# A two-layer hybrid decoder on one core: dropping the meta tokens behind attention and cutting the remaining 1024 into tiles of 256

## The chip, the cores and the metric

The kernel runs on one core of a Trainium2 chip. TensorE (PE in the profile) multiplies 128 x 128 weights, which it loads first (PEld), with a moving operand of up to 512 columns and writes to PSUM, which has eight banks of 512 fp32 columns. VectorE (DVE), ScalarE (ACT) and GpSimd (POOL) do the rest of the arithmetic; SyncE (SP) only issues transfers here. The metric is the device time of one execution in microseconds (us), as the median of several runs.

## The reference, cut to what matters

The input has 1024 tokens of width 1024; 16 learned meta tokens are put in front, which makes 1040. Layer 0 is a state-space mixer and a convolutional gated network (FFN); layer 1 is a stick-breaking attention and an FFN. The meta tokens are dropped at the very end.

```python
h = jnp.concatenate([jnp.broadcast_to(meta_tokens[None], ...), x], axis=1)      # 1040 tokens
h = h + _ssd_mixer(_rmsnorm(h, ssd_norm[0]), ...)
h = h + _conv_ffn(_rmsnorm(h, ffn_norm[0]), ...)
...
o = _stick_breaking_attention(q, k_shared, v_shared).reshape(b, L, SB_WIDTH)
h = h + o @ sb_w_o[j]
h = h + _conv_ffn(_rmsnorm(h, ffn_norm[layer]), ...)
return _rmsnorm(h, final_norm)[:, N_META:]

def _conv_ffn(u, w_up, conv_w, conv_b, w_down):
    h = _causal_dwconv(u @ w_up, conv_w, conv_b)      # three taps: this token and the two in front
    g, val = jnp.split(h, 2, axis=-1)
    return (jax.nn.silu(g) * val) @ w_down
```

Attention reads keys and values of all 1040 tokens. Behind it only the FFN's convolution looks at other tokens: the two in front. So of the meta tokens only the last two have any effect on the output of layer 1's last steps.

## The kernel before

**Numbers and layout.** The stream is held as eight tiles of 128 features x tokens. Each fp32 product is made of three matmuls on split operands (`mm3`, L148): high x high, high x low, low x high, at lines 151 to 153. A matmul line in the profile is therefore mostly one of these three, and the names of its operands tell the stage.

**Tiles of tokens.** The FFN of both layers works on L = 1040 tokens, in four tiles of `FN` = 260 and in halves of 520. The up projection has a halo of `HB` = 2 tokens, so its matmuls have 262 columns.

**Output projection** (`o_proj`, L1405). The attention output of 8 head pairs is read from DRAM and split (`split` in thirds, `split_half` in halves). For each of eight feature blocks, four tiles of 260 are accumulated over 4 or 6 pairs (`accumulate`, L376), whose end is the DVE add at L383.

**Step into the FFN** (`enter_ffn`, L729). The last pairs are added tile by tile; squares are summed by a matmul with ones (`square_row`, L804) to the norm's factors; the stream goes to DRAM (`hm`); `forms` (L814) makes the seven operand sums that the up projection's fast 2 x 2 matrix scheme needs (seven products instead of eight).

**Up projection** (`up`, L896). 22 blocks; each has two halves of tokens with seven products of 4 x 3 matmuls, a three-tap convolution (`conv`, L269), SiLU, a product and a store of 260 tokens to DRAM (`g`).

**Down projection** (`down`, L969). Sixteen of 22 blocks of hidden rows go through the same seven-product scheme, in two rounds of two sets. For each product, `operands` (L1008) of a set are made on DVE, ACT and POOL one set ahead: sums, then splits (`gl` at L1032, `wl` at L1030). A product has eight PSUM tiles (two tiles of 260 tokens x four feature blocks), which take all eight banks by the list `kinds`; a first pass over all eight with set 0, a second with set 1, and behind each tile of the second pass an add to its accumulator (`add`, L1072: DVE at L1077, ACT at L1075 in round 0 for four of the products). The six rows left over are plain products, tile by tile (L1144 on), and meanwhile DVE runs `sums` (L1043), which puts the seven products together.

**The end** (`finish`, L1428; `finish_tokens`, L1441; `finish_last`, L1467). The final norm and the transpose to token rows run per chunk of up to 116 tokens: `down` calls `after(h, j - 1)` behind tile j, so that tokens 0 to 347 leave behind tile 1, tokens 348 to 779 behind tile 2. The last tile's 260 tokens go in chunks of 96, 96 and 68 through `finish_last`, whose `each` runs behind each feature block of tile 3. Transposes go to banks of the tag `sm`, of which there are three.

**Order.** Behind attention no order is written by hand. A scheduler puts each engine's instructions in order by a simulated timeline; where several are ready, the one that the program traced first goes first. PSUM and SBUF tiles of one tag rotate through its buffers. `keep_in_program_order` (L175) puts an activation-table load behind the instruction that ScalarE was given last.

Of the kernel before, what the change touches and what calls it, by code (L numbers as in the profile page):

```python
# [29 lines left out]
FN = 260  # L30
HB = 2
FW = 264

# [33 lines left out]
class Trunk:  # L67
# [87 lines left out]
    def split(self, t, s, eng=None):  # L155

        nc = self.nc
        hi, lo = self.Q(s + "h", F32R), self.Q(s + "l", F32R)
        for s0, n in TT:
            c = slice(s0, s0 + n)  # L160
            nc.scalar.activation(hi[:, c], t[:, c], AF.Copy)
            (eng or nc.vector).tensor_tensor(lo[:, c], t[:, c], hi[:, c].bitcast(F32), op=ALU.subtract)
        return hi, lo

    def split_half(self, t, s):

        x = self.Q(s, F32R)
        hi, lo = x[:, : L // 2], x[:, QW // 2 : QW // 2 + L // 2]
# [560 lines left out]
    def enter_ffn(self, layer, h, last, pool):  # L729


        nc = self.nc
# [6 lines left out]
        def tile(j, work):  # L739
            ws, ops = last[j // 2]  # L740
            ms[j] = self.sm("ms")
            for f in range(KD):
                self.accumulate(h, f, FN * j, FN, lambda i, f: (ws[i][0][:, f * P : f * P + P], ws[i][1][:, f * P : f * P + P]), ops, HB, next(banks), L // 2 * (j // 2))
                self.square_row(ms[j], h, j, f)
                next(work, None)

        def factors(j):

            c = r[:, HB + FN * j : HB + FN * j + FN]
            b, ps = self.tmp("y")[:, :FN], ms.pop(j)[:, :FN]  # L750
# [9 lines left out]
        def rest():  # L760
            forms.append(form_tiles())
            yield from self.forms(h, r, 1, f"ffn_norm{layer}", forms[1], pool)
# [21 lines left out]
        def store(x):  # L784
            for k in range(KD):
                nc.sync.dma_start(d[k, :, L // 2 * x : L // 2 * (x + 1)], h[k][:, HB + L // 2 * x : HB + L // 2 * (x + 1)])
# [8 lines left out]
        work = self.forms(h, r, 0, f"ffn_norm{layer}", forms[0], pool)  # L795
# [8 lines left out]
    def square_row(self, ms, h, j, f):  # L804

        q = self.tmp("sq")[:, :FN]
        self.nc.scalar.activation(q, h[f][:, HB + FN * j : HB + FN * j + FN], AF.Square)
        self.nc.tensor.matmul(ms[:, :FN], self.ones, q, start=f == 0, stop=f == KD - 1, skip_group_check=True)
# [5 lines left out]
    def forms(self, h, r, t, gain, tiles, pool):  # L814


        nc = self.nc
# [78 lines left out]
    def up(self, layer, w0, forms, rest, pool):  # L896

        nc = self.nc
        tt = nc.vector.tensor_tensor
        N = HB + FN  # L900
        cw, cb = f"ffn_conv_w{layer}", f"ffn_conv_b{layer}"
        d = self.dp.tile([KF, P, L], F32, tag=f"g{layer}", name=f"g{layer}")
# [66 lines left out]
    def down(self, layer, gd, hd, pool, after, each=None):  # L969
# [4 lines left out]
        H, S = D // 2, L // 2  # L974
# [97 lines left out]
        def add(i, f, t, ps, first):  # L1072
            x = acc[i, f][:, FN * t : FN * t + FN]
            if first and i in (1, 5, 6, 7):
                nc.scalar.activation(x, ps[:, :FN], AF.Copy)  # L1075
            else:
                self.last_add = tt(x, x, ps[:, :FN], op=ADD)  # L1077
# [35 lines left out]
        for m in range(0, len(plan), 2):  # L1113
# [3 lines left out]
            if r == 0 and i == 7:  # L1117
                for f in range(KD):
                    nc.sync.dma_start(h[f][:, :L] if f < 4 else h[f][:, half(0)], hd[f] if f < 4 else hd[f, :, half(0)])
# [5 lines left out]
            for x in range(2):  # L1125
# [279 lines left out]
    def o_proj(self, hd, od, pool):  # L1405

        a = self.a
        h = [None] * KD
        first = PAIRS - 2

        def part(p, x):
            t = self.Q("o")[:, : L // 2]
            self.nc.sync.dma_start(t, od[p, :, L // 2 * x : L // 2 * (x + 1)])
            return self.split_half(t, "o")

        ops = [self.split(self.fetch(od[p], "o"), "o") for p in range(first - 2)]
        ops = [ops + [part(p, 0) for p in (first - 2, first - 1)], ops]
        for f in range(KD):
            w = self.load_w(a["w_o_f"][f], first * P)
            h[f] = self.fetch(hd[f], "h", front=HB)  # L1420
# [185 lines left out]
```

## Time and profile before

| what | value |
|---|---|
| median of 3 runs (lowest, highest) | 3010.03 us (3007.62, 3012.0) |
| span of the profiled execution | 3005.5 us |
| median of the runs less that span | 4.5 us |
| TensorE busy, mean granted clock | 2887.2 us (96%), 0.986 |
| VectorE, ScalarE, GpSimd busy | 77%, 55%, 44% |

The profile covers one execution, from its first to its last instruction. The 4.5 us between the span and the median of the runs are taken as what lies around the span; the profiled execution's own time is known only through its span. "Idle before" in a row is the time in which the engine stood still just before these instructions, with the instruction that released it. A row that begins with two times is a start and a duration; a row that begins with a window has for each engine the busy time and in brackets the number of instructions.

### The profile page before, as it was taken

To read this page: it belongs to the slowest core of one execution; us is meant where nothing else is said; L and a number is where in the kernel's file an instruction comes from. 1 tells how busy PE (TensorE), PEld (TensorE's weight loads), DVE (VectorE), ACT (ScalarE), POOL (GpSimd) and SP (SyncE) were. 2 spreads that over 40 slices of the span, in tenths; PEclk is the share of its full clock that TensorE was granted. 3 is DMA by queue.
4 is the path that set the end of the run, shared out by engine and by line. 5 is a ranking of instruction groups with operands and counts; after the bars stand their busy time and mean duration, and the time that the engine had idled before them with its cause. 6 is when DMAs were issued, how large, how long until landed. Compare 5 with 4: busy or idle time off the path is not lost. (4 is left out here: it accounts for less than half of the span.)

```text
span 3005.5 us, 58807 instructions
## 1 busy us (share of the span) xinstructions
PE 2887.2 (96%) x22559; PEld 2776.5 (92%) x22559; DVE 2311.1 (77%) x4073; ACT 1657.7 (55%) x3419; POOL 1308.8 (44%) x1260
## 2 busy tenths in 40 slices
PE   7999999989998999999999999999899999999998
PEld 4999898979998999999999999999798999999998
DVE  5587868886369788778966888888749887888875
ACT  4554545553145556555324888887736556555433
POOL 1254444542335666654343222222343666663441
PEclk9999999999999999999999999999999999999999
DMA  5233333323221222235132222222332222225332
GB/s 162 71 106 90 105 97 103 108 63 138 74 82 56 83 73 79 84 107 178 50 128 81 59 67 57 71 61 56 131 114 71 79 75 82 79 75 181 100 100 64
DMA packets 123482, 273.43 MB, mean 91 GB/s; under 512 B 13728, under 2 KB 53280, under 8 KB 123200
## 3 DMA queue, kind: packets, MB, share of 16 engines
q1 hardware_dynamic: 117824, 258.54, 27.7%
q10 hardware_dynamic: 4112, 6.56, 0.7%
q8 instruction: 178, 2.92, 0.4%
q0 software_dynamic: 1264, 4.57, 0.4%
q14 instruction: 104, 0.85, 0.1%
HBM read 201.25 MB, written 53.45 MB: 85 GB/s over the span
## 5 line engine op out<-in xcount | busy, mean ns | idle before, releaser
L151 PE MATMUL pj<-uh,wh 128*128 128x348 f32 (+2 forms) x1536 | 504.7, 329 | 12.2 <-ACT bk L609 6.2
L152 PE MATMUL pj<-ul,wh 128*128 128x348 f32 (+2 forms) x1536 | 497.9, 324 | 0.0
L153 PE MATMUL pj<-uh,wl 128*128 128x348 f32 (+2 forms) x1536 | 495.2, 323 | 0.0
L151 PE MATMUL p<-bh,fh 128*128 128x262 f32 x1408 | 403.5, 287 | 6.6 <-DVE c L276 4.6
L153 PE MATMUL p<-bh,fl 128*128 128x262 f32 x1408 | 403.1, 287 | 3.6 <-POOL fl L882 3.6
L152 PE MATMUL p<-bl,fh 128*128 128x262 f32 x1408 | 402.6, 286 | 0.1
L882 POOL TENSOR_TENSOR fl<-x,fh 128x1024 fp32r<-128x1024 f32 x88 | 212.6, 2417 | 269.4 <-ACT fh L881 176.6
L152 PE MATMUL p<-bl,wh 128*128 128x262 f32 x1056 | 302.8, 287 | 6.2 <-DVE bl L834 6.1
L151 PEld LDWEIGHTS pj<-uh,wh 128*128 128x128 f32 x1536 | 291.1, 190 | 16.1 <-ACT bk L609 6.8
L151 PE MATMUL p<-bh,wh 128*128 128x262 f32 x1056 | 302.6, 287 | 0.9 <-ACT bh L833 0.9
L153 PE MATMUL p<-bh,wl 128*128 128x262 f32 x1056 | 302.4, 286 | 0.0
L276 DVE SCALAR_TENSOR_TENSOR c<-p,params,c 128x260 f32<-128x260 f32 x528 | 251.6, 484 | 56.2 <-ACT c L273 46.7
L152 PEld LDWEIGHTS pj<-ul,wh 128*128 128x128 f32 x1536 | 291.5, 190 | 1.8 <-issue 1.0
L153 PEld LDWEIGHTS pj<-uh,wl 128*128 128x128 f32 x1536 | 291.2, 190 | 1.0 <-issue 0.8
L145 POOL TENSOR_TENSOR wl<-w,wh 128x1024 fp32r<-128x1024 f32 (+2 forms) x76 | 155.8, 2052 | 311.7 <-ACT wh L144 311.7
L151 PEld LDWEIGHTS p<-bh,fh 128*128 128x128 f32 x1408 | 268.5, 191 | 7.6 <-ACT c L273 4.9
L153 PEld LDWEIGHTS p<-bh,fl 128*128 128x128 f32 x1408 | 269.1, 191 | 4.2 <-POOL fl L882 4.1
L152 PEld LDWEIGHTS p<-bl,fh 128*128 128x128 f32 x1408 | 269.0, 191 | 0.8 <-DVE bl L834 0.5
L152 PE MATMUL acc<-gl,wh 128*128 128x260 f32 x896 | 254.7, 285 | 12.1 <-DVE gl L1032 12.1
L151 PE MATMUL acc<-gh,wh 128*128 128x260 f32 x896 | 250.8, 284 | 8.2 <-DVE p L1077 7.7
L153 PE MATMUL acc<-gh,wl 128*128 128x260 f32 x896 | 253.4, 285 | 0.0
L923 DVE TENSOR_TENSOR c<-c,c 128x260 f32<-128x260 f32 x176 | 240.9, 1370 | 4.4 <-ACT c L919 1.4
(326 smaller groups left out, 8456.6 us busy)
## 6 DMA issues: line engine op xcount, KB each, us to landing
w<-in_w_up SPq DMA_DIRECT2D x88, 512.0 KB
g<-c SPq DMA_DIRECT2D x176, 130.0 KB
w<-in_w_down SPq DMA_DIRECT2D x44, 512.0 KB
w<-in_w_in SPq DMA_DIRECT2D x40, 512.0 KB
b<-g SPq DMA_DIRECT2D x32, 520.0 KB
E<-ea_d SPq DMA_DIRECT2D x32, 464.0 KB
D<-acs_d SPq DMA_DIRECT2D x32, 420.5 KB
h<-h_d SPq DMA_DIRECT2D x16, 520.0 KB
```

The source lines that it names most:

```text
L145: nc.gpsimd.tensor_tensor(wl[:, :n], w32[:, :n], wh[:, :n].bitcast(F32), op=ALU.subtract)
L151: mm(out, wh, uh, start=first, stop=False, skip_group_check=joins)
L152: mm(out, wh, ul, start=False, stop=False, skip_group_check=joins)
L153: mm(out, wl, uh, start=False, stop=last, skip_group_check=joins)
L276: nc.vector.scalar_tensor_tensor(out, ps[:, o + i : o + i + n], wcol(i), out, op0=ALU.mult, op1=ALU.add)
L882: tt(lo[:, :n], t, hi[:, :n].bitcast(F32), op=ALU.subtract)
L923: self.last_up = tt(g[:, :FN], g[:, :FN], v[:, :FN], op=ALU.mult)
```

## The change

Layer 1's steps behind attention work on tokens 16 to 1039 alone (1024), with the two tokens in front as a lead. A class `Tokens` holds the numbers of each layer; layer 0 keeps its 1040 tokens, tiles of 260 and halves of 520.

- Output projection and step into the FFN: attention output and stream are read from token 14 on; tile 0 has 258 columns (256 and the lead), the others 256. The lead takes the place of the two zero columns in front.
- Up projection: tiles of 256 with the halo of two, 258 columns.
- Down projection: each product works on the whole half of 512 tokens in one matmul where there were two of 260. A product has four PSUM tiles instead of eight, and products alternate between the first four and the last four entries of `kinds`. The plain products behind it have tiles of 256.
- End: chunks of 128 tokens. Tile j leaves behind tile j + 1, for j = 0, 1 and 2; the call for tile 2 is traced behind the last tile's accumulations and `finish_last`. The last tile has two chunks of 128. Each chunk is one store. Each second half of a chunk's row goes over ScalarE and GpSimd, where before a call's third chunk went over VectorE alone.

```diff
+class Tokens:
+    def __init__(self, at, lead):
+        self.at, self.lead = at, lead
+        self.n = L - at
+        self.half, self.tile = self.n // 2, self.n // 4
+        self.wide = [(t, self.tile) for t in (0, self.tile)] if self.half > 512 else [(0, self.half)]
+    def span(self, j):
+        a = self.lead if j == 0 else 0
+        return self.tile * j - a, self.tile + a
+    def part(self, x):
+        a = self.lead if x == 0 else 0
+        return self.half * x - a, self.half + a
+FFN = Tokens(0, 0), Tokens(META, HB)
...
     def enter_ffn(self, layer, h, last, pool):
-        nc.gpsimd.tensor_copy(r[:, :HB], self.zero[:, :HB])
-        d = self.dp.tile([KD, P, L], F32, tag=f"hm{layer}", name=f"hm{layer}")
+        if not g.lead:
+            nc.gpsimd.tensor_copy(r[:, :HB], self.zero[:, :HB])
+        d = self.dp.tile([KD, P, g.n], F32, tag=f"hm{layer}", name=f"hm{layer}")
...
     def up(self, layer, w0, forms, rest, pool):
+        FN = FFN[layer].tile
...
     def down(self, layer, gd, hd, pool, after, each=None):
-        H, S = D // 2, L // 2
+        FN, S, H = FFN[layer].tile, FFN[layer].half, D // 2
+        wide = FFN[layer].wide
...
-                c, e = slice(q * H + f * P, q * H + f * P + P), slice(FN * t, FN * t + FN)
-                self.mm3(ps[:, :FN], wh[:, c], wl[:, c], gh[:, q, e], gl[:, q, e], first and q == 0, not first and q == 1)
+                s0, n = wide[t]
+                c, e = slice(q * H + f * P, q * H + f * P + P), slice(s0, s0 + n)
+                self.mm3(ps[:, :n], wh[:, c], wl[:, c], gh[:, q, e], gl[:, q, e], first and q == 0, not first and q == 1)
...
-                for n, (t, f) in enumerate((t, f) for t in range(2) for f in range(4)):
+                for n, (t, f) in enumerate((t, f) for t in range(len(wide)) for f in range(4)):
                     if x == 0:
-                        ps[t, f] = kinds[n]("acc")
+                        ps[t, f] = kinds[(m // 2 * 4 * len(wide) + n) % 8]("acc")
...
     def o_proj(self, hd, od, pool):
+        at, n = g.at - g.lead, g.n + g.lead
+        def fetch(src, s):
+            t = self.Q(s)
+            self.nc.sync.dma_start(t[:, :n], src[:, at:])
+            return t
...
-            t = self.Q("o")[:, : L // 2]
-            self.nc.sync.dma_start(t, od[p, :, L // 2 * x : L // 2 * (x + 1)])
+            s0, m = g.part(x)
+            t = self.Q("o")[:, :m]
+            self.nc.sync.dma_start(t, od[p, :, g.at + s0 : g.at + s0 + m])
...
-        ops = [self.split(self.fetch(od[p], "o"), "o") for p in range(first - 2)]
+        tiles = [(n // 3 * i, n // 3) for i in range(3)]
+        ops = [self.split(fetch(od[p], "o"), "o", tiles=tiles) for p in range(first - 2)]
...
     def finish(self, h, j):
-        if j < 2:
-            self.finish_tokens(h, CH[3 * j : 3 * j + 3])
-        if j == 1:
-            self.finish_tokens(h, [(CH[6][0], 3 * FN - CH[6][0])])
+        if j < 3:
+            self.finish_tokens(h, [(t, P) for t in range(FFN[1].tile * j, FFN[1].tile * (j + 1), P)])
...
     def finish_tokens(self, h, chunks):
-                if b and i < 2:
+                if b:
                     nc.scalar.activation(y[:m, w], p[:m], AF.Copy, scale=r[:m, i : i + 1])
                     nc.gpsimd.tensor_tensor(y[:m, w], y[:m, w], self.gfin[:m, w], op=ALU.mult)
...
-            self.store(y, t0, m)
+            nc.sync.dma_start(self.a["out"][t0 : t0 + m, :], y)
...
     def finish_last(self):
-        M = 96
-        chunks = [(0, M), (M, M), (2 * M, FN - 2 * M)]
+        FN = FFN[1].tile
+        chunks = [(o, P) for o in range(0, FN, P)]
```

More of the change, by code (lines that the diff above doesn't have):

```diff
@@ L794, in enter_ffn @@
         forms = [form_tiles()]
[L795 removed]
+        work = self.forms(layer, h, r, 0, forms[0], pool)
         for j in (2, 3):
@@ L802, in enter_ffn, with square_row, forms @@
         return d, ws0 + next(w0), forms, rest()
[L804 to L808, printed above, removed]
+    def square_row(self, ms, h, f, s0, n):
+        q = self.tmp("sq")[:, :n]
+        self.nc.scalar.activation(q, h[f][:, HB + s0 : HB + s0 + n], AF.Square)
+        self.nc.tensor.matmul(ms[:, :n], self.ones, q, start=f == 0, stop=f == KD - 1, skip_group_check=True)
     def ft(self, pool, s="ft"):
         return pool.tile([P, FW], F32, tag="ft", name=self.nm(s), bufs=NFT)
-    def forms(self, h, r, t, gain, tiles, pool):
-        nc = self.nc
+    def forms(self, layer, h, r, t, tiles, pool):
+        nc, gain, FN = self.nc, f"ffn_norm{layer}", FFN[layer].tile
         N, N2 = HB + FN, HB + 2 * FN
@@ L1496, in block @@
                 a, e = (x * P for x in done)
-                for p, y, (o, m) in zip(ps, ys, chunks):
-                    nc.vector.tensor_tensor(y[:m, a:e], p[:m, a % 512 : a % 512 + e - a], self.gfin[:m, a:e], op=ALU.mult)
+                for p, y in zip(ps, ys):
+                    nc.vector.tensor_tensor(y[:, a:e], p[:, a % 512 : a % 512 + e - a], self.gfin[:, a:e], op=ALU.mult)
         def each(h, f):
```

62 lines of the change are left out of this document (29 added, 33 removed).

## The prediction

> **What bounds the kernel now.** I read the page's busy shares first, then the busy time of each engine in the stages behind attention, then the list of matmul starts for the time from one matmul to the next, then TensorE's waits, and last the end of the run, instruction by instruction.
>
> ```profile
> span 3005.5 us, 58807 instructions
> PE 2887.2 (96%) x22559; PEld 2776.5 (92%) x22559; DVE 2311.1 (77%) x4073; ACT 1657.7 (55%) x3419; POOL 1308.8 (44%) x1260
> ```
>
> TensorE (PE) has something in flight 96% of the span. Everything up to the end of attention stays as it is, so only the stages behind it count. They are, by the windows below: output projection, the step into the gated network, the up projection, the seven products of the down projection, its plain rest with the final norm, and the tail (columns: us, then busy us and instructions of PE, PEld, DVE, ACT, POOL, then granted clock, DMA share, GB/s).
>
> ```profile
> 2171.00:2275.00 104.00, 103.83 (x817) 101.75 (x817) 57.33 (x125) 41.58 (x83) 40.43 (x24) 1.00 0.35 121
> 2275.00:2310.00 35.00, 28.45 (x181) 26.67 (x181) 34.11 (x78) 19.85 (x47) 8.05 (x7) 0.85 0.13 49
> 2310.00:2741.00 431.00, 429.17 (x3524) 428.99 (x3523) 348.12 (x554) 251.53 (x509) 283.05 (x162) 1.00 0.29 94
> 2741.00:2912.00 171.00, 161.12 (x1316) 159.88 (x1315) 138.17 (x144) 72.62 (x96) 81.21 (x32) 0.98 0.33 108
> 2912.00:2996.00 84.00, 82.38 (x698) 81.76 (x697) 58.11 (x123) 25.28 (x53) 13.45 (x14) 1.00 0.17 53
> 2996.00:3005.50 9.50, 1.00 (x12) 0.92 (x10) 2.84 (x11) 2.35 (x5) 0.00 (x0) 0.64 0.39 112
> ```
>
> PE sets the pace of 104 + 431 + 84 us of this; the 35 us belong to VectorE (DVE, 34.11 busy); the 171 us are mixed: PE lacks 10 us, and DVE has work for 138. No stage comes near the DMA engines' limit (0.35 at most).
>
> The busy time of a matmul says little, since neighbours overlap. What counts is the distance of starts. Back to back, by the first and last starts of unbroken runs and one window:
>
> ```profile
> 2927.96 0.28 PE L151 MATMUL acc<-g,fh 128*128 128x260 f32 x1
> ...
> 2947.38 0.28 PE L151 MATMUL acc<-g,fh 128*128 128x260 f32 x1
> ```
> ```profile
> 412.34 0.32 PE L153 MATMUL pj<-uh,wl 128*128 128x348 f32 x1
> ...
> 415.66 0.32 PE L153 MATMUL pj<-uh,wl 128*128 128x348 f32 x1
> 415.81 0.32 PE L151 MATMUL pj<-uh,wh 128*128 128x344 f32 x1
> ...
> 419.40 0.32 PE L153 MATMUL pj<-uh,wl 128*128 128x344 f32 x1
> ```
> ```profile
> 2350.00:2700.00 350.00, 350.00 (x2874) 1.00 0.25 78
> ```
>
> 260 columns: nine groups of 18 in 19.42 us, 119.9 ns. 348 columns: 21 steps in 3.32 us, 158.1 ns. 344: 23 steps in 3.59 us, 156.1 ns. 262 (the up projection): 350 us / 2874 = 121.8 ns. From 260 to 348 a column costs 38.2 / 88 = 0.434 ns, and some 7 ns belong to the matmul itself. The two columns from 260 to 262 cost 1.9 ns, as much as the four from 344 to 348.
>
> **The change, term by term.** (a) Up projection: 22 blocks x 2 halves x 7 products x 12 = 3696 matmuls go from 262 to 258 columns. No row has 258. At 0.434 ns a column the gain is 1.7 ns each, 6.4 us; at the price of its nearest row, 260, 1.9 ns, 7.0 us; at 0.95 ns a column, which 260 to 262 taken alone would say, 14 us. I take **7.0**. The stage is PE's (429 of 431 us), and DVE, ACT and POOL work on tiles 1.5% shorter as well.
>
> (b) Down products: 7 products x 2 rounds x 2 sets x 8 tiles x 6 = 1344 matmuls of 260 become 672 of 512. No row has such a back-to-back 512. By the line through 260 and 348 it costs 119.9 + 252 x 0.434 = 229.3 ns, and a pair saves 239.8 - 229.3 = 10.5 ns: **7.1 us**. If the cost were purely by columns (512/260 x 119.9 = 236.1) it would be 2.5 us; by the line through 262 and 348 (0.422 ns a column, so 158.1 + 164 x 0.422 = 227.3) it would be 8.4 us. I take the first line, since its two ends are plain runs of one length.
>
> The Trainium skill, "TensorE: Matmul & The Clock Gate", section "Back-to-back issue gap", has two rules here: N/2.4 + 2.5 ns for a matmul by itself, and about 81 ns (N=128) and 131 ns (N=512) in streams where each has its weight load. By the first a pair saves 2 x 110.8 - 215.8 = 5.9 ns, 4 us in all; by a line through the second 2 x 98 - 131 = 65 ns, 44 us. The measured 119.9 ns at 260 lies above both; the measured slope is near the first rule's.
>
> (c) Waits in the same stage. TensorE's waits from 2735 to 2926 us, and the groups behind them:
>
> ```profile
> PE acc L152 <- DVE gl L1032: 5.8, 3, 4.0
> PE acc L151 <- DVE p L1077: 3.8, 2, 2.2
> PE acc L151 <- DVE h L383: 1.6, 1, 1.6
> PE acc L151 <- DVE h L1077: 0.2, 1, 0.2
> ```
> ```profile
> L1032 DVE TENSOR_TENSOR gl<-b,gh 128x1040 fp32r<-128x1040 f32 x26 | 48.5, 1867 | 15.2 <-ACT gh L1031 10.9 <-PE acc L152 3.0 <-PE acc L153 1.1
> L1077 DVE TENSOR_TENSOR h<-h,acc 128x260 f32<-128x260 f32 x51 | 19.0, 416 | 7.7 <-PE acc L153 7.7
> L1077 DVE TENSOR_TENSOR p<-p,acc 128x260 f32<-128x260 f32 x24 | 8.8, 413 | 0.0
> L1498 DVE TENSOR_TENSOR y<-fin,gfin 96x512 f32<-96x512 f32 x2 | 1.4, 686 | 0.9 <-PE fin L1492 0.9
> ```
>
> The L1077 waits are for a PSUM bank: a product's eight tiles take all eight banks, so each tile of the next product waits until DVE has added up its predecessor one product ago. With four tiles that alternate between the two halves of the banks, the predecessor is two products old, about 22 us of PE work instead of 11. I expect these 4.0 us to go, and the L383 wait (DVE busy with sums of 520 columns, now 512) to stay; bounds 0 and 5.6. But DVE's operands remain: L1032 shrinks only from 1040 to 1024 elements. The adds help a little: 80 on DVE of 415 ns become 40, at 686 ns by the L1498 row, which also reads PSUM: 40 x (830 - 686) = 5.8 us less DVE work. So DVE has 138 - 6 - 1.5 = 130 us to do in a stage that PE would now finish in about 171 - 7 - 4 = 160: 81% as before. Where the first adds of a product come later (a tile is closed after 12 long matmuls, not 12 short ones) or an operand is late, PE waits for L1032 more than the 5.8 us of now. I set **4.0 back to 0.4** for that, that is, 3.6 us of the gain of (b) and (c) is given back; bounds 0 (all kept) and 11 (all of it).
>
> (d) Output projection and the step behind it: 768 matmuls of 260 become 256 (a quarter of them 258) in a stage that is PE's: 576 x 1.7 + 192 x 0.9 = **1.1 us**. Its loads start 14 tokens into a row and are 4104 bytes instead of 4160: at a DMA share of 0.35 they hide behind the projection's earlier blocks; if they did not, the first of them would stop PE by one load's delay, under 2 us. Eight copies of a zero halo leave POOL, which has 40 of 104 us to do.
>
> (e) The last part of the down projection: 576 matmuls from 260 to 256, **1.0 us**. The stretches that DVE bounds (35 us, and some 25 at the start of the down stage) shorten by 1.5%: **0.9 us**.
>
> (f) The end. Now tokens leave in chunks of 116 rows (seven before the last tile, three in it); afterwards eight of 128. By the groups from 2926 us on and the last instructions:
>
> ```profile
> L1459 PE MATMUL fin<-ident,h 128*116 128x128 f32 x48 | 6.9, 273 | 0.0
> L1464 DVE SCALAR_TENSOR_TENSOR y<-fin,ty,gfin 116x512 f32<-116x512 f32 x8 | 5.7, 746 | 1.5 <-PE fin L1459 1.4
> L1462 POOL TENSOR_TENSOR y<-y,gfin 116x512 f32<-116x512 f32 x4 | 5.2, 1291 | 8.1 <-ACT y L1461 8.1
> L1450 PE MATMUL fs<-one,sq 128*116 128x1 f32 x24 | 2.7, 227 | 0.0
> ```
> ```profile
> 2994.40 0.37 PE L153 MATMUL acc<-g,wl 128*128 128x260 f32 x1
> 2996.07 0.93 PE L1509 MATMUL fs<-one,sq 128*96 128x1 f32 x10
> 2998.28 0.16 DVE L208 TENSOR_TENSOR ty<-ty,tb 96x3 f32<-96x3 f32 x1
> 2998.48 1.95 ACT L1513 ACTIVATE y<-y,ty 96x512 f32<-96x512 f32 x3 [0.81 <-DVE ty L208]
> 3000.18 0.34 DVE L1515 TENSOR_SCALAR y<-y,ty 68x256 f32<-68x256 f32 x1
> 2959.71 42.55 SPq L357 DMA_DIRECT2D out<-y  x18
> ```
>
> 80 transposes become 64. Eight x4 take 6.9 us overlapped, about 0.11 us of PE each by their starts: 1.8 us saved; 40 column sums become 32, about 0.1 each: 0.8 us. But the third tile's finish moves: it was traced ahead of the last tile's accumulations and now stands behind them and behind the last tile's own finish. What moves past: eight squares and two activations on ACT with a table load, its sums and five small steps on DVE, two sums on POOL, 8 sum and 16 transpose instructions on PE (2.5 us), four evacuations (two DVE, two ACT followed by POOL) and two stores on SP. Squares and their sums find room while the last tile accumulates. PE has none: accumulations traced earlier go first, as the chunks' transposes now cut into later accumulations. So the last accumulation ends 1.8 + 0.8 + 2.5 = 5.1 us earlier, and behind it this work runs beside the last tile's: the sums 0.75 us in, and, with one free bank of three, the four evacuations one after another, behind which come two POOL products of 1.29 us. Counting these, the last store is ready 8.5 us behind the last accumulation, where now it is 3000.5 - 2994.4 = 6.1; four stores become one at the very end, which I put at 0.7 us less. Net **-3.3 us** (5.1 - 2.4 + 0.7 = 3.4, rounded down); bounds -1 and -5. If the work did find a gap earlier, the end shortens by its last chunks instead, and the sum is the same within 1 us.
>
> Sum: 7.0 + 7.1 + 4.0 - 3.6 + 1.1 + 1.0 + 0.9 + 3.3 = 20.8, and I keep **20** us. Span 3005.5 - 20 = 2985.5. The median of the runs is 3010.0, 4.5 above the span; with that around it, **2990** us.
>
> **Rivals.** *Down stage held by DVE*: PE's shorter products only wait longer for L1032. For it: DVE at 81%, three waits already. Against: 33 us of DVE idle time. Then (b) and (c) bring nothing: 20 - 7.5 = 12.5 gained, 2997.5. *Columns or weights count otherwise*: 262 to 258 saves 3.8 ns (7 us more). Or a weight load sets the pace:
>
> ```profile
> L152 PEld LDWEIGHTS acc<-gl,wh 128*128 128x128 f32 x438 | 83.6, 191 | 6.5 <-DVE gl L1032 6.5
> ```
>
> If 512 columns cost no more than these 191 ns, a pair saves 49 ns, 33 us instead of 7, and the time is 2964. Against: 348 columns take 38 ns more than 260 with the same loads. The stream rule quoted above is of this kind. *Slower*: with four long tiles per product, each pair of operands that DVE finishes late stops PE. There are 14 products; now the first three of them wait 4.0, 0.4 and 1.4 us. If each waited 2.9 us, 14 x 2.9 - 5.8 = 34.8 us would stand against a gain of 23.6 (the 20 without the 3.6 given back): 11 us slower than before, 3021. It decides from (23.6 + 5.8) / 14 = 2.1 us a product. Against: products beyond the third have no L1032 wait at all now, and their operands are made a product ahead. *Nothing gained*: a new order of all instructions behind attention costs by chance what the shorter matmuls bring; nothing in the profile speaks for 20 us of it, but 15 would do.
>
> **Chances.** Forecast (2981 to 2995): 0.62. Down stage held: 0.18 (to 3003). Columns or weights otherwise: 0.10 (2963 to 2981). Nothing gained: 0.05. Slower: 0.05. A measurement of this kernel tells about 0.2%, 6 us, from no change, so the first three count as faster: 0.90, 0.05, 0.05. The range 2980 to 3001 holds the first two cases nearly whole.
>
> **What would show it.** Right: up-stage matmuls 119 to 120 ns apart; down products 225 to 232 ns apart; no L1077 wait of PE; the third tile's transposes behind the last accumulation. Wrong: L1032 waits of PE above 13 us in the down stage; 512-column starts above 236 ns; more than 10 us between the last accumulation and the last store's data.

## The result, and the profile after

The changed kernel takes 3001.3 us (median of nine runs, 2997.84 to 3004.22), the kernel before 3009.9 us (nine runs beside them); the ratio is 0.9977 with a 95% interval of 0.9967 to 0.9987. The forecast was a gain of 20 us; 8.6 were measured, and 3001.3 lies just above the range.

From the page of the changed kernel, the busy times:

```profile
span 2998.0 us, 57316 instructions
PE 2881.1 (96%) x21863; PEld 2737.4 (91%) x21863; DVE 2303.7 (77%) x4026; ACT 1646.3 (55%) x3403; POOL 1309.6 (44%) x1250
```

The span fell by 7.5 us. Where, is read from the first matmul of each stage. From the list of matmul starts of the kernel before (its last accumulation, at 2994.40, is in the prediction), then of the changed kernel:

```profile
2270.52 0.48 PE L151 MATMUL p<-bh,fh 128*128 128x262 f32 x1
...
2738.54 0.28 PE L151 MATMUL acc<-gh,wh 128*128 128x260 f32 x1
...
2913.17 0.28 PE L151 MATMUL acc<-g,fh 128*128 128x260 f32 x1
```
```profile
2269.03 0.47 PE L171 MATMUL p<-bh,fh 128*128 128x258 f32 x1
...
2731.92 0.39 PE L171 MATMUL acc<-gh,wh 128*128 128x512 f32 x1
...
2900.84 0.28 PE L171 MATMUL acc<-g,fh 128*128 128x256 f32 x1
...
2980.60 0.28 PE L173 MATMUL acc<-g,wl 128*128 128x256 f32 x1
```

| stage | before, us | after, us | difference | forecast |
|---|---|---|---|---|
| up to the first up matmul | 2270.5 | 2269.0 | -1.5 | -1.1 |
| up projection | 468.0 | 462.9 | -5.1 | -7.0 |
| seven products of the down projection | 174.6 | 168.9 | -5.7 | -7.5 |
| plain rest, to the last accumulation | 81.2 | 79.8 | -1.5 | -6.1 |
| tail, from there to the end | 11.1 | 17.4 | +6.3 | +1.7 |

The forecast for the rest is the 1.0 us of shorter matmuls and the 5.1 us by which (f) let the last accumulation come earlier; that for the tail is the 2.4 us later last store less the 0.7 us for fewer stores. The 0.9 us of shorter VectorE stretches in (e) belong to no single row, and the rounding down took as much off the forecast. So of the 12.5 us that are missing, 4.6 each are in the plain rest and the tail, and nearly 2 each in the up projection and the products.

Windows of the changed kernel (columns as in the prediction): the plain rest, the middle of the up projection, and two stretches of 20 us at the start of the products.

```profile
2900.80:2981.00 80.20, 76.10 (x641) 75.25 (x639) 51.87 (x105) 19.38 (x40) 14.24 (x11) 1.00 0.16 59
...
2350.00:2700.00 350.00, 349.89 (x2906) 349.71 (x2905) 290.84 (x453) 198.05 (x414) 242.80 (x140) 1.00 0.25 79
2731.90:2751.90 20.00, 15.11 (x61) 11.89 (x60) 18.54 (x15) 7.56 (x11) 9.00 (x3) 0.90 0.65 230
2751.90:2771.90 20.00, 16.99 (x62) 13.30 (x61) 18.68 (x12) 8.52 (x11) 8.62 (x3) 0.85 0.00 1
```

Up: 350 us / 2906 = 120.4 ns a matmul, where it was 121.8. TensorE stands still for 4.1 us in the rest, where in the kernel before it did for 1.6 (84.00 less 82.38 us in the prediction's window). An unbroken run of long matmuls in the list of starts has 194 rows, the first and the last of which are

```profile
2773.18 0.39 PE L172 MATMUL acc<-gl,wh 128*128 128x512 f32 x1
...
2817.95 0.39 PE L173 MATMUL acc<-gh,wl 128*128 128x512 f32 x1
```

that is, 44.77 us / 193 = 232.0 ns for 512 columns. TensorE's waits from the first product to the last accumulation (us in total, times, longest):

```profile
PE acc L172 <- DVE gl L1057: 7.9, 2, 4.9
PE acc L171 <- DVE h L403: 2.3, 1, 2.3
PE acc L173 <- POOL wl L1113: 1.3, 1, 1.3
PE acc L171 <- DVE h L1104: 0.5, 1, 0.5
```

The waits for a bank of a product (3.8 us for p and 0.2 for h before) are gone; the one that L1104 still ends is in the plain rest. The stops for `gl` (a product's split operand) are two instead of three and 2.1 us longer in sum. Two stops in the rest are new, for `wl` and for the last product's add. The tail, in order of time:

```profile
2980.60 0.28 PE L173 MATMUL acc<-g,wl 128*128 128x256 f32 x1
...
2981.37 0.42 ACT L1508 ACTIVATE sq<-h 128x256 f32<-128x256 f32 x1 [1.94 <-DVE h L403]
...
2981.69 2.54 ACT L239 ACTIVATE sq<-h 128x256 f32<-128x256 f32 x8
...
2982.71 0.16 DVE L222 TENSOR_SCALAR fs<-fs 128x2 f32<-128x2 f32 x1 [1.37 <-PE fs L1535]
...
2984.25 1.28 ACT L195 ACT_TABLE_LOAD   x1
2984.39 1.48 DVE L245 TENSOR_TENSOR sq<-sq,sq 128x256 f32<-128x256 f32 x3
2985.55 0.20 ACT L223 ACTIVATE ty<-fs 128x2 f32<-128x2 f32 x1
...
2992.76 1.26 POOL L1490 TENSOR_TENSOR y<-y,gfin 128x512 f32<-128x512 f32 x1 [0.62 <-ACT y L1489]
```

All eight squares of the third tile (L239) run behind the last tile's last square (L1508), though the third tile's stream was complete 21 us earlier (its last add ended at 2960.25) and ScalarE had just stood still for 1.94 us. The last tile's own logarithm (L223, 2985.55) had its operand at 2982.87, but waited behind these squares and a table load. The last store's data is ready at 2994.02, 13.4 us behind the last accumulation; 6.1 were before and 8.5 forecast, and more than 10 was one of the prediction's signs of being wrong.

### The profile page after: what moved, and what is told of

It reads as the page before. It is cut to its first block, busy times and chain, and to the rows that moved or that the text cites. A ratio compares the mean times of both kernels' runs of the same rounds, so it can differ in the third digit from the quotient of the medians.

```text
span 2998.0 us, 57316 instructions
## 1 busy us (share of the span) xinstructions
PE 2881.1 (96%) x21863; PEld 2737.4 (91%) x21863; DVE 2303.7 (77%) x4026; ACT 1646.3 (55%) x3403; POOL 1309.6 (44%) x1250
## 5 line engine op out<-in xcount | busy, mean ns | idle before, releaser
L171 PE MATMUL p<-bh,fh 128*128 128x262 f32 (+1 forms) x1408 | 401.4, 285 | 6.8 <-DVE c L296 2.8
L173 PE MATMUL p<-bh,fl 128*128 128x262 f32 (+1 forms) x1408 | 401.6, 286 | 3.4 <-POOL fl L905 3.4
L172 PE MATMUL p<-bl,fh 128*128 128x262 f32 (+1 forms) x1408 | 402.4, 286 | 0.1
L172 PE MATMUL p<-bl,wh 128*128 128x262 f32 (+1 forms) x1056 | 301.2, 285 | 6.2 <-DVE bl L857 6.1
L171 PE MATMUL p<-bh,wh 128*128 128x262 f32 (+1 forms) x1056 | 302.4, 287 | 0.9 <-ACT bh L856 0.9
L173 PE MATMUL p<-bh,wl 128*128 128x262 f32 (+1 forms) x1056 | 301.3, 285 | 0.0
L296 DVE SCALAR_TENSOR_TENSOR c<-p,params,c 128x260 f32<-128x260 f32 (+1 forms) x528 | 250.4, 481 | 47.3 <-ACT c L293 36.9
L947 DVE TENSOR_TENSOR c<-c,c 128x260 f32<-128x260 f32 (+1 forms) x176 | 242.0, 1377 | 5.0 <-ACT c L943 2.0
L1055 POOL TENSOR_TENSOR wl<-w,wh 128x1024 fp32r<-128x1024 f32 x56 | 147.5, 2637 | 207.9 <-ACT wh L1054 205.7
L172 PE MATMUL acc<-gl,wh 128*128 128x260 f32 (+1 forms) x672 | 217.9, 325 | 14.7 <-DVE gl L1057 14.7
```

The lines of the kernel that those rows point to most:

```text
L171: mm(out, wh, uh, start=first, stop=False, skip_group_check=joins)
L172: mm(out, wh, ul, start=False, stop=False, skip_group_check=joins)
L173: mm(out, wl, uh, start=False, stop=last, skip_group_check=joins)
L296: nc.vector.scalar_tensor_tensor(out, ps[:, o + i : o + i + n], wcol(i), out, op0=ALU.mult, op1=ALU.add)
L947: self.last_up = tt(g[:, :FN], g[:, :FN], v[:, :FN], op=ALU.mult)
L1055: pt(wl, y, wh.bitcast(F32), op=SUB)
```

## The experiments

All are edits of the changed kernel. Each row has its own runs and its ratio to the kernel before on the same chip; the stage lengths are of its profiled execution, cut as above. The changed kernel was profiled a second time, to see how far stages vary by themselves.

| run | median, us | ratio, 95% interval | products | plain rest | tail |
|---|---|---|---|---|---|
| changed kernel | 3001.3 | 0.9977 (0.9967 to 0.9987) | 168.9 | 79.8 | 17.4 |
| changed_again | 3002.0 | 0.9982 (0.9973 to 0.9991) | 170.7 | 80.6 | 17.0 |
| own_squares | 2998.3 | 0.9960 (0.9944 to 0.9976) | 169.1 | 79.0 | 13.5 |
| one_table | 2998.9 | 0.9966 (0.9954 to 0.9978) | 170.0 | 80.5 | 16.3 |
| third_early | 2997.8 | 0.9962 (0.9947 to 0.9977) | 171.0 | 82.8 | 9.6 |
| two_256 | 3004.8 | 0.9993 (0.9982 to 1.0004) | 176.9 | 75.7 | 17.3 |
| no_alternation | 3000.5 | 0.9972 (0.9962 to 0.9982) | 172.7 | 75.9 | 17.4 |
| tokens_behind | 3001.3 | 0.9976 (0.9967 to 0.9986) | 167.9 | 79.9 | 17.0 |
| weights_other_queue | 3001.4 | 0.9975 (0.9963 to 0.9987) | 168.8 | 79.3 | 17.0 |
| sums_paced | 2997.9 | 0.9969 (0.9959 to 0.9979) | 168.8 | 77.0 | 17.6 |
| early_paced_tokens | 2995.9 | 0.9963 (0.9950 to 0.9975) | 169.4 | 78.4 | 9.7 |
| operands_first | 2988.4 | 0.9930 (0.9917 to 0.9942) | 163.4 | 78.7 | 9.7 |

The first up matmul, in front of which all of these are the same program, came between 2265.2 and 2273.0 us in their profiles. A span or a median therefore moves by some us for reasons ahead of every edit; the stage lengths tell the edits apart, the medians confirm only the larger ones. The rest varies for one more reason: in five profiles (changed_again, one_table, third_early, tokens_behind and up_248) the mean clock over it is 0.98, in the others 1.00. In these five TensorE ran at half speed for 3.4 us just behind its wait for the first add of the rest, which makes the rest 1.7 us longer.

**changed_again.** No edit.

> The changed kernel itself, with the kernel before on the same chip, for the spread of the stages between profiles of one program: up projection 462 to 464 us, products 168 to 171, plain rest 79 to 81, tail 17 to 17.8, and the time 2999 to 3003 us.

The stages agree within 2 us, the up projection at 464.6.

### What makes the tail long

**own_squares.** The third tile's eight squares take buffers of another tag; the order in which the program traces the work is unchanged.

```diff
-                q = self.tmp("sq")
+                q = self.ft(own, "sq") if own else self.tmp("sq")
...
-        accs = self.square_sum([h[k][:, s0 : s0 + n] for k in range(KD)], n, D)
+        accs = self.square_sum([h[k][:, s0 : s0 + n] for k in range(KD)], n, D, self.pool1 if s0 == 512 else None)
```

> The third tile's eight squares get buffers of their own (the tag of the operand sums, which are done by then); everything else, and the order in which the program traces it, is as in the changed kernel. Buffer theory: the squares stood behind the last tile's only because buffers of one tag are handed out in traced order; now they run while the last tile accumulates, the table load in front of the third tile's factors leaves the tail with them, and the span from the last accumulation to the end falls from 17.4 us to 11 to 13.5; the time is 2995 to 2998. Rival, the evacuations: what is long behind the last accumulation is sixteen transposes, four evacuations and four stores one after another; the tail stays at 16 to 17.5 and the time at 3000 to 3002.

ScalarE's instructions in order of time in this run:

```profile
2962.43 0.42 ACT L239 ACTIVATE sq<-h 128x256 f32<-128x256 f32 x1 [1.71 <-DVE h L403]
2962.86 1.28 ACT L195 ACT_TABLE_LOAD   x1
...
2983.45 0.42 ACT L1508 ACTIVATE sq<-h 128x256 f32<-128x256 f32 x1 [1.94 <-DVE h L403]
2985.21 0.30 ACT L223 ACTIVATE ty<-fs 128x2 f32<-128x2 f32 x2 [1.34 <-DVE fs L222]
```

The third tile's last square is now at 2962.43, as soon as its block was there, and 21 us ahead of the last tile's last square. The table load has gone forward with the squares, and both tiles' logarithms run together. The tail is 13.5 us, the last store's data ready 9.5 us behind the last accumulation. Nothing but the tag of a buffer was changed, so the squares had waited for buffers: those of a tag are handed out in the order in which the program asks, and the last tile's squares ask first. The rival (evacuations one after another, whatever the squares do) falls for about 4 us, and keeps the 2.4 us that 13.5 still is above the kernel before.

**one_table.** The table load is left out in front of the second and third tile's factors.

```diff
-        r = self.token_rstd(ss, P, len(chunks), 0.0, src=pss)
+        r = self.token_rstd(ss, P, len(chunks), 0.0, y=self.small("ty") if s0 else None, src=pss)
```

> The activation-table loads in front of the second and the third tile's factors are left out (the table is there since the first tile's); the squares stay behind the last tile's. Buffer theory: the 1.28 us load holds up the last tile's own logarithm by up to 2.8 us, but the third tile's squares and sums still come late; the tail falls from 17.4 to 14.6 to 16.1 us. Rival, the table: the load alone makes the tail long, which falls to 11 to 13.5 us.

The tail is 16.3 us, 0.7 to 1.1 below the two profiles of the changed kernel and a little above what was expected: the load alone costs no more than its own 1.28 us, and not the 4 us.

**third_early.** The third tile's finish is traced behind that tile, ahead of the last tile.

```diff
-                res = after(h, j - 1, res)
+                if not each or j < 3:
+                    res = after(h, j - 1, res)
+                if each and j == 2:
+                    res = after(h, 2, res)
```

> The third tile's finish is traced behind that tile, ahead of the last tile's accumulations, as in the kernel before. Buffer theory: the third tile's 2.5 us of TensorE work go back in front of the last accumulation (the plain rest 80.0 to about 82.5 us), and the tail falls from 17.4 to 9 to 11 us; the time is 2995 to 2998. Rival, the chunks: two last chunks of 128 rows, each one store, make the end long by themselves; the tail stays above 14 us and the time at 3000 or above.

The tail is 9.6 us, 1.5 below the kernel before: chunks of 128 rows make a shorter end, as long as only the last tile's are in it. The rest is 3.0 us longer than in the changed kernel's first profile, and 2.2 longer than in its second, which has the same 1.7 us of slower clock in the rest as this one; the 2.2 us are about the 2.5 us of TensorE work that the move had taken out of it. Rest and tail together are 92.4 us here, 92.5 in own_squares and 97.2 in the changed kernel: either cure of the late squares brings 4.7 to 4.8 us.

### What takes the rest's gain

**two_256.** Only the long matmuls are undone.

```diff
-        self.wide = [(t, self.tile) for t in (0, self.tile)] if self.half > 512 else [(0, self.half)]
+        self.wide = [(t, self.tile) for t in (0, self.tile)]
```

> Only the long matmuls are undone: each down product has two tiles of 256 columns for each feature block again, so eight tiles in all eight banks, one product's after the other's. Forecast's theory: 1344 matmuls of 118.2 ns take 4.1 us more than 672 of 230.4 ns, and TensorE waits for banks about 4 us again; the products' stage goes from 168.7 to 174 to 178 us. Rival, VectorE holds the stage: what TensorE takes longer it waits less for operands; the stage stays at 167 to 171 us.

TensorE's waits of this run, from the products to the end of the rest:

```profile
PE acc L172 <- DVE gl L1057: 7.0, 3, 4.3
PE acc L171 <- DVE p L1104: 3.5, 2, 2.1
PE acc L171 <- DVE h L1104: 1.8, 2, 1.6
PE acc L171 <- DVE c L296: 1.4, 1, 1.4
PE acc L171 <- DVE h L403: 0.9, 1, 0.9
```

The bank waits are back (5.3 us in L1104), and the products take 8.0 us more, as the forecast's theory says. What neither theory had is the rest: 75.7 us, 4.1 less than in the changed kernel, with 0.9 us of waits for h (L403) instead of 2.3 and none for `wl`. So half or more of what the long matmuls gain is given back behind the products (4.1 of 8.0 us by the first profile of the changed kernel, 4.9 of 6.2 by the second).

**no_alternation.** Each product takes the first four banks of the list.

```diff
-                        ps[t, f] = kinds[(m // 2 * 4 * len(wide) + n) % 8]("acc")
+                        ps[t, f] = kinds[n]("acc")
```

> Each down product takes the same first four banks of the list instead of the first and the last four in turn, so that its tiles wait for the adds of the product just before. Forecast's theory: the bank waits of the kernel before come back, 2 to 5 us of them, and the products' stage goes from 168.9 to 171 to 174 us. Rival: the four tiles give VectorE 4.2 us between a tile's end and its bank's next use, enough for an add of 0.7 us; no bank wait, 168 to 170 us, and the alternation bought nothing.

The products' waits for banks are 2.3 us (1.6 for p, 0.7 for h), and the products take 172.7 us, 3.8 more than in the first profile of the changed kernel and 2.0 more than in the second. The rest is again 75.9 us, and the median, 3000.5, is that of the changed kernel. Alternating the banks works and buys nothing here, since the rest waits for what the products save.

**tokens_behind.** VectorE stood still for 5.42 us at 2904.20 in the changed kernel, for the load of rows that are needed 40 us later; three adds and all sums stood behind. The edit puts these splits behind the last add.

```diff
-                tt(lo, lo.bitcast(F32), hi.bitcast(F32), op=SUB)
+                sub = tt(lo, lo.bitcast(F32), hi.bitcast(F32), op=SUB)
+                if each and x:
+                    behind(sub, self.last_add, "behind the products")
```

> Only VectorE's two splits of the second half's first rows (L1124 in the changed kernel, started at 2904.20 us after 5.42 us of standing still for their load) are put behind the last add of the products. Late-operand theory: they blocked three adds and all the sums behind them, although the second half isn't needed for another 40 us; without them the sums start 4 to 6 us earlier, VectorE's 5.4 us stop and TensorE's waits for h (L1104 0.5 and L403 2.3 us) go, and the plain rest falls from 79.8 to 76 to 78 us; the stop for wl (1.3 us) stays. Rival, too much work on VectorE: the sums are simply longer than TensorE's first tile; the L403 wait stays above 1.5 us and the rest at 79 to 80 us.

The stop and the L1104 wait went, but the L403 wait is 2.3 us as before, and the rest 79.9. VectorE's first sums and the first adds of the rest in this run:

```profile
2899.03 5.66 DVE L1074 TENSOR_TENSOR p<-p 128x512 f32<-128x512 f32 x4
...
2911.24 1.07 DVE L403 TENSOR_TENSOR h<-h,acc 128x256 f32<-128x256 f32 x3
```

The sums began 1.6 us into the rest (6.4 in the changed kernel), the first add of the rest still came 13.8 us into it. That the rest didn't get shorter is in part the clock, which fell behind this wait (1.7 us). But the wait itself stayed, though the operands were no longer in front: as its cause, the late operands fall.

**weights_other_queue.** The loads of the plain rest's weights go over POOL's queue, so that the loads of token rows on SP's don't stand behind them.

```diff
-            nc.sync.dma_start(w32, a["w_down"][layer, b])
+            (nc.gpsimd if each else nc.sync).dma_start(w32, a["w_down"][layer, b])
```

> Only the five loads of the plain rest's weights and the one before them move from SP's queue to POOL's own, so that the loads of token rows no longer stand behind a load that waits for POOL to free its buffer. Late-operand theory: the token rows land 4 to 8 us earlier, VectorE's 5.4 us stop goes, and the plain rest falls from 79.8 to 76 to 78 us. Rival, POOL: the weights' own way (load, copy, split on POOL) sets the start of the rest; the wl stop grows above 1.3 us and the rest stays at 79 us or above.

VectorE's stop in front of the sums fell from 5.42 to 2.37 us, and the sums began 4.1 us into the rest (6.4 in the changed kernel), but the first add came 14.7 us into it. The rest is 79.3 us, with an L403 wait of 3.0 and 0.4 for `wh`; the 1.3 us for `wl` are gone. No gain that can be told from the spread: late loads were not it.

**sums_paced.** In the changed kernel the order on VectorE is this, from the stop to the first adds of the rest:

```profile
2904.20 0.69 DVE L1124 TENSOR_TENSOR g<-g 128x512 fp32r<-128x512 f32 x1 [5.42 <-ACT g L1123]
...
2907.20 3.50 DVE L1074 TENSOR_TENSOR p<-p 128x512 f32<-128x512 f32 x4
2910.62 1.88 DVE L1074 TENSOR_TENSOR h<-h,p 128x512 f32<-128x512 f32 x3
...
2916.04 0.40 DVE L403 TENSOR_TENSOR h<-h,acc 128x256 f32<-128x256 f32 x1
```

The rest has five banks in turn and one block of 2.1 us per bank: after 10.7 us TensorE needs the first bank again, but eleven sums stand in front of the add that frees it, at 2916.04, 15.2 us into the rest. The edit lets each sum follow the add that was traced just ahead of it.

```diff
-                        behind(tt(acc[x, f], acc[x, f], acc[y, f], op=ADD), self.last_add, "behind the products")
+                        behind(tt(acc[x, f], acc[x, f], acc[y, f], op=ADD), self.acc_add if each else self.last_add, "behind the products")
```

> Only the order on VectorE changes: each of the sums that put the seven products together comes behind the add of the plain rest's feature block that was traced just ahead of it, so that eleven sums no longer stand in front of the first block's add. Order theory: the five banks of the plain rest's first blocks were full (five blocks of 2.1 us) before VectorE came to the first add, 15.2 us into the rest, because a fixed order has eleven sums and four splits ahead of it, and TensorE's earlier arrival only made it wait there; now the L403 wait goes from 2.3 to under 0.5 us and the plain rest from 79.8 to 77 to 78 us, the wl wait (1.3 us) stays. Rival, too much work on VectorE: the sums don't fit beside the first two tiles at all, so the wait only moves to a later add; the waits for h stay at 2 us or more and the rest at 79 us or above.

TensorE's waits of this run over the same stretch, then the first add of the rest:

```profile
PE acc L172 <- DVE gl L1057: 7.9, 2, 4.8
PE acc L173 <- POOL wl L1113: 1.5, 1, 1.5
PE acc L171 <- DVE h L1104: 0.2, 1, 0.2
...
2913.17 0.42 DVE L403 TENSOR_TENSOR h<-h,acc 128x256 f32<-128x256 f32 x1
```

The wait for L403 is gone, although VectorE has the same work to do, and the first add comes 8.6 us into the rest. The rest is 77.0 us, 2.8 to 3.6 less than in the two profiles of the changed kernel. The rival (too much work on VectorE) falls; it was the order. In two_256 and no_alternation TensorE came to the rest 8.0 and 3.8 us later, counted from the first product, and found more of that work done.

### What a column costs in the up projection

**up_248.** Nine of twelve matmuls of each product in layer 1's up projection take 248 columns instead of 258, which leaves ten columns of each tile with a part of their sum.

```diff
-                    self.mm3(ps[:, :N], wh[:, c], wl[:, c], *forms[t][0][i][k], start and k == 0, k == KD // 2 - 1, not start)
+                    n = N - 10 if layer and k else N
+                    self.mm3(ps[:, :n], wh[:, c], wl[:, c], *(x[:, :n] for x in forms[t][0][i][k]), start and k == 0, k == KD // 2 - 1, not start)
```

> In layer 1's up projection the last three quarters of each product's matmuls (9 of 12) take 248 columns instead of 258, so that ten columns lack part of their sum. By the slope of 0.434 ns a column the mean distance in the middle of the stage falls from 120.4 to 117.2 ns (9/12 x 4.34) and the stage by 12.0 us; by the 0.34 ns a column that 262 to 258 measured, to 117.9 ns and by 9.4 us. Should something else than TensorE hold the stage, it shortens by less than 5 us.

```profile
2350.00:2650.00 300.00, 300.00 (x2585) 300.00 (x2584) 255.06 (x402) 171.78 (x369) 219.30 (x124) 1.00 0.25 82
```

By this window of the run a matmul takes 300 / 2585 = 116.05 ns on average, 4.39 less than in the changed kernel (120.44), and the stage 448.3 us, 14.6 less; the median is 2987.1 us. The twelve matmuls lost 9/12 x 10 = 7.5 columns on average, so that is 4.39 / 7.5 = 0.59 ns a column, more than either price expected, where 262 to 258 gave 1.34 / 4 = 0.34. So it is TensorE that sets the time of this stage, and no single price per column fits its widths. Why is open.

### Together

**early_paced_tokens.** The edits of third_early, sums_paced and tokens_behind at once.

> Three edits together: the third tile's finish traced behind that tile, the sums behind the adds, and the second half's first splits behind the products' last add. If the tail and the order of the rest are what was lost, the tail is 9 to 11 us, the plain rest 79.5 to 81.5 us (its 2.5 us of transposes and sums are back in it), and the time 2993 to 2996 us. If third tile and plain rest draw on the same slack, it is 2996 to 2999, no better than the third tile's edit alone.

Rest 78.4 and tail 9.7 us, 9.1 us less than in the changed kernel in these two stages, where third_early alone had 4.8: the two losses are separate. The median is 2995.9 us.

**operands_first.** The three edits of early_paced_tokens, and in the first round two preparations are put behind the splits that TensorE waits for.

```diff
-                    tt(a21, a22, a21, op=SUB)
-                    tt(b11, b11, b12, op=ADD)
+                    behind(tt(a21, a22, a21, op=SUB), self.last_gl, "behind the operands before")
+                    behind(tt(b11, b11, b12, op=ADD), self.last_gl, "behind the operands before")
```

> The three edits of the run before, and in the first round of products the two preparations of the third product (L1042 and L1043 of the changed kernel) put behind the splits of the second product's operands, since one of them stood in front of the split that TensorE waited 4.9 us for and took 3.36 us. Order theory: the two stops for gl fall from 7.7 to 2 to 5 us, the products' stage from 169.4 to 164 to 167 us, and the time is 2990 to 2994. Rival, VectorE's work: the preparations are only late a product later; the stops stay at 7 us or more in sum, and the time at 2994 to 2998.

TensorE's waits of this run, then the window of its products:

```profile
PE acc L172 <- DVE gl L1060: 4.8, 2, 2.9
PE acc L173 <- POOL wl L1116: 1.0, 1, 1.0
```
```profile
2735.86:2899.30 163.44, 158.47 (x675) 127.11 (x674) 140.91 (x109) 70.62 (x82) 85.33 (x31) 0.99 0.32 109
```

The stops for `gl` fell from 7.7 us (early_paced_tokens) to 4.8, the products from 169.4 to 163.4, a little more than expected, and the rival falls. The stops are 2.9 us of these 6.0; the other 3 go with the clock, whose mean in this stage went from 0.96 to 0.99 (about 5 us, but part of the slow time had fallen into the stops themselves). At 2988.4 us, ratio 0.9930 (0.9917 to 0.9942), this version is faster than both kernels, and close to the 2990 that the forecast had put down for the change by itself.

## Why the prediction was wrong

Small slips first, which don't move the forecast gain. The 4.5 us taken as lying around the span are mostly spread between runs. The profiled execution of the changed kernel took 2999.73 us with a span of 2998.0, 1.7 us more. The DMA share of at most 0.35 is that of the stages ahead of the tail; the tail's row in the same window list has 0.39. The 6.9 us of transposes in (f) are 48, twelve times four and not eight. And 2 x 110.8 - 215.8 is 5.8, not 5.9.

(a) *Up projection, 7.0 us.* Mis-sized: 5.1 us (3.4 by the second profile of the changed kernel, whose stage is 464.6). The mechanism held, 3696 shorter matmuls in a stage that is TensorE's. The price came from the 260 columns of another stage; 258 cost 120.4 ns here, not 119 to 120. The rival's 3.8 ns for 262 to 258 falls: it is 1.34 ns.

(b) *Products of 512, 7.1 us.* Mis-sized: 232.0 ns instead of 229.3, so a pair saves 7.8 ns and 672 of them 5.2 us. It lies between the line through 260 and 348 and the purely proportional price, inside the bounds. The stream rule of the Trainium skill ("TensorE: Matmul & The Clock Gate", section "Back-to-back issue gap") gives 131 ns at 512 columns; the measurement decides against it, and against the rival of its kind, by which 512 columns would have cost no more than a weight load's 191 ns.

(c) *Bank waits, 4.0 us gained and 3.6 given back.* The bank waits went, and two_256 and no_alternation brought them back, so that mechanism is shown. What was given back inside the products, 2.1 us of longer `gl` stops, is part of what was meant. The sum left out what follows a stop: TensorE's clock. Over the first 40 us of the stage it was granted 0.90 and 0.85 of its speed (rows above), 2.0 and 3.0 us lost. In the kernel before, the windows of the same stretches are

```profile
2738.50:2758.50 20.00, 16.00 (x120) 15.79 (x119) 19.51 (x16) 9.18 (x17) 9.38 (x4) 0.86 0.66 230
2758.50:2778.50 20.00, 18.15 (x144) 17.74 (x144) 20.00 (x11) 10.07 (x18) 10.87 (x4) 0.97 0.09 27
```

or 3.4 us in all. Where the clock was slow while TensorE stood still anyway (1.3 us of the changed kernel's stretch, 1.8 of the kernel before's, at half speed), nothing was lost; that leaves about 4.4 and 2.5 us, so the clock took some 1.9 us more than before. Shorter matmuls 5.2, bank waits 4.0, longer stops -2.1 and the clock -1.9 make 5.2 of the 5.7 us measured.

(d) *Output projection, 1.1 us.* The 1.5 us measured can't be told from the spread of 2265.2 to 2273.0.

(e) and (f), *the plain rest, 6.1 us earlier at its end; measured 1.5.* This step failed. The shorter matmuls and the work moved out are there: two_256, which keeps both, has a rest of 75.7 us, near the forecast (81.2 - 6.1 = 75.1). But the prediction looked for what the faster products give back only among their own operands, and put the rest's waits down as unchanged. Behind the products, a fixed order on VectorE put eleven sums in front of the first add, and a TensorE that came 5.7 us sooner than before, counted from the first product, waited there for 2.3 us. With the stops for `wl` and for the products' last add it stood still for 4.1 us, where it had been 1.6: that is 2.5 of the 4.6 us that are missing. sums_paced removed the wait for the first add and brought the rest to 77.0 us; what keeps it 1.9 us above 75.1 is open. The rival "down stage held by VectorE" had the right engine, but not the place, and it was order and not the amount of work.

(f) *The tail, 1.7 us longer; measured 6.3.* "Squares and their sums find room while the last tile accumulates" failed. ScalarE had the room, but the squares had no buffers, and the table load that is pinned behind them came between the last tile's sums and its logarithm. With buffers of their own the last store's data is ready 9.5 us behind the last accumulation, near the 8.5 forecast. The step named order on TensorE (traced earlier goes first), and this was right for the transposes; it didn't ask the same of the buffers. The other points of (f) held: no transposes of the third tile ahead of the last accumulation, and a shorter way from the last store's data to the end (4.0 us, before 5.0).

## What to carry to other kernels

When work is traced later, ask of every resource that is handed out in traced order, scratch buffers too, who now asks first: an idle engine is no room if its output buffer belongs to someone ahead. When a stage gets faster, look past it for the first place where a slower engine's fixed order meets the faster one; here half of a shown gain was lost there, and reordering the slower engine, with the same work, gave 2.8 to 3.6 us back. And a stop of two or three us can be dearer than its length, here by 1.7 us each time the clock fell for 3.4 us behind it.

## What the runs showed of the hardware that was not expected

**The clock behind a stop.** Starts of the changed kernel's long matmuls behind its first stop:

```profile
2749.04 0.80 PE L172 MATMUL acc<-gl,wh 128*128 128x512 f32 x1 [4.89 <-DVE gl L1057]
...
2750.06 0.63 PE L171 MATMUL acc<-gh,wh 128*128 128x512 f32 x1
...
2754.32 0.53 PE L171 MATMUL acc<-gh,wh 128*128 128x512 f32 x1
...
2754.93 0.40 PE L173 MATMUL acc<-gh,wl 128*128 128x512 f32 x1
```

From 2750.06 to 2754.32 ten steps take 0.43 us each, then 0.23 again: about half speed for some 5 us, which costs over 2 us on top of the stop. The changed kernel's second stop, of 3.01 us, was followed by 3.4 us at half clock. In operands_first a stop of 2.90 us was followed by 3.4 us at 0.43 us a step, one of 1.92 us by none. The Trainium skill, "TensorE: Matmul & The Clock Gate", section "HAM oscillation — how this bites in real kernels", lets the clock fall behind gaps of more than about 3.4 us; the trace agrees for 4.89 and 1.92 us, but the stops of 3.01 and 2.90 us are shorter than that, and there the measurement decides.

Near 2.3 us the same stop goes either way. TensorE waited 2.29 us for the first add of the rest in both profiles of the changed kernel. In the first the granted clock over the rest is 1.00 (window above); in the second it was, just behind the wait,

```profile
2919.40:2922.81 3.41, 3.41 (x18) 3.41 (x17) 3.41 (x9) 0.00 (x0) 0.00 (x0) 0.50 0.00 0
```

What decides between the two was not tried.

**VectorE beside GpSimd.** Two equal subtractions of the changed kernel, the second while POOL works:

```profile
2738.86 1.22 DVE L1040 TENSOR_TENSOR b<-b,b 128x1024 f32<-128x1024 f32 x1
...
2740.16 6.60 POOL L1055 TENSOR_TENSOR wl<-w,wh 128x1024 fp32r<-128x1024 f32 x2 [4.34 <-ACT wh L1054]
2741.13 3.44 DVE L1040 TENSOR_TENSOR b<-b,b 128x1024 f32<-128x1024 f32 x1
```

1.22 us become 3.44. It would also explain why the four sums that tokens_behind moved forward, into POOL's weight splits, took 5.66 us there and 3.50 in the changed kernel. The Trainium skill, "SBUF — State Buffer", section "Who interferes with whom", says that a VectorE instruction with two SBUF inputs contends with a GpSimd instruction that reads SBUF; the trace agrees. That this contention is the whole cause of the longer times was not tried.
